# Hybrid decoder layer on one NeuronCore: values projected with the tokens moving, three heads' keys turned by VectorE blocks, turned tiles passed through DRAM

## The chip, the cores and the metric

The kernel is one launch on one core of a Trainium2 chip. The metric is the device time of that core in microseconds, as the median of several runs; before the change it is 2129.17 us over 3 runs (2129.09 to 2129.24). Beside the timed runs there is one profiled execution with its trace, in which every instruction has a line number of the kernel's source. Times of single instructions come from that execution.

## The reference

The layer works on x of 2048 tokens by 1024 features, in float32. The first part mixes tokens with two groups of heads, the second is a gated MLP with a causal convolution, and everything ends in an RMSNorm. The change touches only the first group of heads (HGRN2, a linear recurrence with four heads of key and value width 128) and the transposes that it and the attention use:

```python
u = rmsnorm(h, norm_mix_w[l])
proj = u @ w_in[l]
hq, hf, hi, hg, att = jnp.split(proj, [...], axis=-1)
f = lb + (1.0 - lb) * jax.nn.sigmoid(hf)
k_hg = (1.0 - f);  q_hg = hq * HG_DK ** -0.5;  v_hg = hi
# per head:  S_t = diag(f_t) S_{t-1} + k_t v_t^T,   o_t = S_t^T q_t
o_hg = rmsnorm(hgrn2_chunkwise(q_hg, k_hg, v_hg, log_f), hg_norm_w[l]) * silu(hg)
o_att = sliding_window_attention_with_sinks(aq, ak, av, sinks[l])
h = h + concat([o_hg, o_att]) @ w_out[l]
```

So for each head there are keys K, queries and values v over all tokens. Within chunks of 128 tokens the kernel computes products of queries and keys, and it carries a 128×128 state from chunk to chunk, for which it needs the product of a chunk's keys and values with the tokens as the summed axis.

## The kernel before

**Tiling.** The tokens are worked in two halves of 1024 (`hf` 0 and 1), each as 8 chunks of 128. Activations lie feature by token, 128 features on the partitions and 1024 tokens along the row, and there are 8 such tiles for the 1024 features. Every large product is made of three matmuls on values split into a high and a low part (`hi`, `lo`): high by high, high by low, low by high. `prep` loads a 512 KB weight tile, ACT casts the high part (line 199) and VectorE subtracts to get the low part (line 200).

**Units.** `unit` (line 203) projects the 1024 tokens of a half onto 128 output features: the weights are the stationary operand and 512 tokens move at a time, which makes 8 × 3 × 2 = 48 matmuls into two PSUM banks (line 218). Gates, forget gates (`f`), queries (`hq`), attention projections (`q`, `kv`) and the output projection (`pop`) are such units. There are four `mm` banks in PSUM, and two each of `hg` and `at`.

**Values.** `project_v` (line 670) is not a unit. It takes two heads at once, and here the tokens are stationary, so that its result has tokens on the partitions: for each of the 8 chunks, 24 matmuls with 256 weight columns moving (lines 681 to 683, tile `pvv`). ACT scales each chunk and head with the tokens' inverse norm while it copies them out of PSUM (line 685).

**A head.** `hgrn` (line 485) is a generator with five stages. `f` and `q` are units; `l` runs seven levels of pairwise products in the chunks (tiles `plev`, lines 546 to 596), in which VectorE multiplies K and Q in place after each level (lines 564, 565, 575, 576; K is final after the last line 576); `s` transposes the eight chunks of K on TensorE (tile `pkn`, line 607), copies them out with ACT (line 608, tile `Kn`, tokens on the partitions), multiplies them with the values (tile `pu`, line 614) and adds up the states (line 621); `p` makes the outputs (tile `po`, lines 634 and 639) with v and the states, and normalizes them. `gate` (line 521) is the gate's unit, run later.

**Turned tiles.** For three of the four heads the normalized output, and for three of the four attention pairs the attention weights, are transposed by `turned` (line 335) and not by TensorE: VectorE transposes all 32×32 blocks of a 128×1024 tile in one instruction (line 338), and 16 DMAs of 32 KB from SBUF to SBUF put the blocks in place (line 341). This is done for 12 tiles of attention weights and 6 of outputs.

**Order.** The stages of heads and pairs are interleaved by a list, `ORDER` (line 40): `f q l s p` are a head's stages, `qa sc pv pw` an attention pair's, `v` a `project_v`, `g` a gate, `m` a split for the output projection. A planner then lays out each engine's own instruction list when the kernel is built, from the program's order, its own costs for the instructions and the buffers that are free; on the chip each engine runs its list from front to back. All DMAs named here are issued by SyncE's queue (SP), in its list's order. Tiles with one tag share a fixed number of buffers: `t4` (2) holds Kn, the outputs and their turned form, `pp` (3) attention tiles and their turned form, `v` (2) the values.

Of the kernel before, what the change touches and what calls it, by code (L numbers as in the profile page):

```python
# [8 lines left out]
F32 = mybir.dt.float32  # L9
# [8 lines left out]
P = 128  # L18
# [20 lines left out]
UP_AFTER = 'T2'  # L39
ORDER = ("f0 q0 l0 qa0 v0 sc0 s0 p0 f1 q1 pv0 pw0 l1 qa1 sc1 f2 s1 p1 q2 pv1 pw1 l2 qa2 v1 sc2 f3 s2 p2 q3 pv2 "  # L40
         "pw2 l3 qa3 sc3 s3 p3 pv3 pw3 g0 g1 m4 m5 m6 g2 m0 m1 g3 m7 m2 m3").split()
LEVELS = [1, 2, 4, 8, 16, 32, 64]
# [3 lines left out]
VB = 2  # L46
TURNED_PAIRS = 3
TURNED_HEADS = 3


@with_exitstack
def hymba_layer(ctx: ExitStack, tc: tile.TileContext, a: dict, out: bass.AP, rows_out: bass.AP):
# [281 lines left out]

    def turned(p, tag, bufs, src, dst):

        t = p.tile([P, 4, 8, 32], F32, tag=tag, name="turn", bufs=bufs)
        nc.vector.transpose(t, src.rearrange("p n (c j) -> p c n j", j=32))
        for a in range(4):
            for c in range(4):  # L340
                nc.sync.dma_start(dst[32 * c:32 * c + 32, a], t[32 * a:32 * a + 32, c])

# [40 lines left out]
    def attend(hf, j, X, invb, KS, V, VD, mix, p):  # L383
# [9 lines left out]
        for g in range(NB):  # L393
# [48 lines left out]
            if j < TURNED_PAIRS:  # L442
                pt = p.tile([P, 4, 8, 32], F32, tag="sc", name="pt", bufs=2)
                turned(p, "pp", 3, sc.rearrange("p a b c -> p (a b) c"), pt)
                sc = pt
# [39 lines left out]
    def hgrn(hf, h, X, invb, vs, WG, gates, mix, p, fu=None):  # L485
# [114 lines left out]
        kept = TT if hf + 1 < NH else TT - 1  # L600
        Kn = p.tile([P, TT, P], F32, tag="t4", name="Kn", bufs=2)
        for b in range(NB):
            pk = ps("hg", "pkn")
            n = min(4, kept - 4 * b)
            for i in range(n):
                c = slice((b * 4 + i) * P, (b * 4 + i + 1) * P)
                nc.tensor.transpose(pk[:, i * P:(i + 1) * P], K[:, c], ident)
            nc.scalar.copy(Kn[:, 4 * b:4 * b + n].rearrange("p a b -> p (a b)"), pk[:, 0:n * P])
        SS = p.tile([P, TT, P], F32, tag="SS", name="SS", bufs=1)
        for b in range(NB):  # L610
            pu = ps("hg", "pu")
            for c in range(4 * b, min(4 * b + 4, kept)):
                i = c % 4
                marks["pu"] = nc.tensor.matmul(pu[:, i * P:(i + 1) * P], Kn[:, c], v[:, c], start=True, stop=True)
            for c in range(4 * b, min(4 * b + 4, kept)):
                i = c % 4
                if hf == 0 and c == 0:
                    nc.vector.tensor_copy(SS[:, 0], pu[:, 0:P])
                    continue
                prev = state[:, h] if c == 0 else SS[:, c - 1]  # L620
                nc.vector.scalar_tensor_tensor(SS[:, c], prev, F[:, c:c + 1], pu[:, i * P:(i + 1) * P],
                                               op0=ALU.mult, op1=ALU.add)
# [6 lines left out]
        for b in range(NB):  # L629
            at = [po[b][:, i * P:(i + 1) * P] for i in range(4)]  # L630
            empty = hf == 0 and b == 0
            for i in range(4):
                for k in range(2):
                    marks["po"] = nc.tensor.matmul(at[i][rows(k)], ST[:, k, 4 * b + i], v[:, 4 * b + i],
                                                   start=i == 0, stop=empty and i == 0, skip_group_check=True)
# [15 lines left out]
        if h < TURNED_HEADS:  # L651
            turned(p, "t4", 2, on, q.rearrange("p (a c q) -> p a c q", a=4, c=TT))
        for b, bs in halves() if h >= TURNED_HEADS else ():
# [15 lines left out]

    def project_v(hf, pr, X, rs, p):  # L670

        v = [p.tile([P, TT, P], F32, tag="v", name="v", bufs=VB) for _ in range(2)]
        parts = [prep(a["w_v"][pr, s]) for s in range(2)]
        for tt in range(TT):
            o = ps("mm", "pvv")
            t = slice(tt * P, (tt + 1) * P)
            for kt in range(KT):
                hi, lo = parts[kt // 4]
                xh, xl = X[kt]
                c = slice((kt % 4) * 256, (kt % 4 + 1) * 256)  # L680
                nc.tensor.matmul(o[:, 0:256], xh[:, t], hi[:, c], start=kt == 0, stop=False)  # L681
                nc.tensor.matmul(o[:, 0:256], xl[:, t], hi[:, c], start=False, stop=False)  # L682
                nc.tensor.matmul(o[:, 0:256], xh[:, t], lo[:, c], start=False, stop=kt == KT - 1)  # L683
            for i in range(2):
                nc.scalar.activation(v[i][:, tt], o[:, i * P:(i + 1) * P], AF.Identity, scale=rs[:, tt:tt + 1])
        return v
# [467 lines left out]
    for hf in range(NH):  # L1154
        X, kv, invb, rs, f0 = nxt
        with ExitStack() as st:
# [7 lines left out]
            for name in ORDER:  # L1164
# [9 lines left out]
                elif stage == "v":  # L1174
                    vs += project_v(hf, n, X, rs, p)
                else:
                    M[n] = split(mix[n], C.hgw if n < TURNED_HEADS else None)
# [9 lines left out]
def _layout(i):  # L1187
# [3 lines left out]
    def cols(w, idx):  # L1191
# [12 lines left out]
    w_out = i["w_out"][0][np.concatenate(rows)]  # L1204
    w_v = np.stack([cols(w_in, 1024 + pr * 256 + ar(256)).reshape(P, 2, D).transpose(1, 0, 2) for pr in range(2)])
    conv = np.concatenate([i["conv_w"][0], i["conv_b"]], 0)
# [5 lines left out]
        "w_f": np.stack([cols(w_in, 512 + h * P + ar(P)) for h in range(4)]),  # L1212
        "w_v": w_v,
        "w_g": np.stack([cols(w_in, 1536 + h * P + ar(P)) for h in range(4)]),
# [39 lines left out]
```

## Time and profile before

| | before |
|---|---|
| median of 3 runs | 2129.17 us |
| the profiled execution's own time | 2129.44 us |
| its span, first to last instruction | 2127.7 us |
| granted TensorE clock | 0.999 |
| TensorE busy (matmuls) | 2113.7 us, 99% |
| VectorE busy | 1632.4 us, 77% |
| ScalarE (ACT) busy | 1050.0 us, 49% |
| DMA | 264.34 MB, mean 124 GB/s |

The time of an execution is its span and about 1.7 us around it. "Busy" is the time in which at least one instruction of an engine was under way. Matmuls overlap each other, so the duration of one (285 to 390 ns) is longer than the distance from one to the next; the pace is read from the starts, or from the rows of the chain of waits, where each stretch of time is counted once. PE is TensorE's matmul side, PEld its weight loads, DVE VectorE, ACT ScalarE, SP SyncE and its DMA queue (SPq in rows). The mixing part of the first half runs from about 33 us to 345 us of the span, that of the second from about 1085 us to 1411 us; the rest is the MLP.

### The profile page before, as it was taken

How to read it: one execution, taken by the hardware profiler on the slowest of the kernel's cores; microseconds unless marked ns; L12 is line 12 of the kernel's file. 1: busy time of each engine (PE TensorE's matmuls, PEld its weight loads, DVE VectorE, ACT ScalarE, POOL GpSimd, SP SyncE). 2: the span in 40 equal slices, each digit the busy share in tenths (PEclk: the TensorE clock that was granted, in tenths of full speed). 3: DMA queues.
4: the chain of work that ended last, by engine and by line, in shares of the span. 5: the costliest groups of instructions: out<-in, count | busy, mean ns of one | idle time of the engine just before them, and what ended most of it. 6: DMA issues, size and time to landing. Idle time of an engine off the chain costs nothing.

```text
span 2127.7 us, 30275 instructions
## 1 busy us (share of the span) xinstructions
PE 2113.7 (99%) x11575; PEld 1763.0 (83%) x11575; DVE 1632.4 (77%) x2427; ACT 1050.0 (49%) x1855; POOL 16.9 (1%) x43
## 2 busy tenths in 40 slices
PE   8999999999999999999999999999999999999998
PEld 6988888888888888888889898888888888888887
DVE  6587786798887878785865776867988788887765
ACT  5455645564444445335635456555544444453353
POOL 2000000000000000000000000000000000000000
PEclk9999999999999999999999999999999999999999
DMA  4121213413232335964641212242223323259644
GB/s 162 42 59 45 68 52 102 136 59 121 91 124 92 98 116 168 379 235 150 216 143 40 61 38 64 60 146 97 80 99 103 110 90 124 94 194 403 228 149 134
DMA packets 105810, 264.34 MB, mean 124 GB/s; under 512 B 15808, under 2 KB 28608, under 8 KB 105664
## 3 DMA queue, kind: packets, MB, share of 16 engines
q1 hardware_dynamic: 105232, 262.14, 36.6%
q8 instruction: 91, 1.49, 0.3%
q14 instruction: 55, 0.45, 0.1%
q10 hardware_dynamic: 432, 0.27, 0.0%
HBM read 195.56 MB, written 57.34 MB: 119 GB/s over the span
## 4 chain that ended last, share of the span: by engine, by line
PE 97%; DVE 2%; DMA 1%; ACT 0%; issue 0%; SPq 0%; ACTq 0%; DVEq 0%
PE X L818 7%; PE X L816 7%; PE X L817 7%; PE pop L218 7%; PE hq L218 4%; PE q L218 4%; PE g L218 4%; PE f L218 4%; PE Y L817 4%; PE Y L818 4%; PE Y L816 4%; PE pdx L1004 3%; PE pdx L1003 3%; PE pdx L1005 3%; PE pdy L1004 3%; PE pdy L1003 3%
## 5 line engine op out<-in xcount | busy, mean ns | idle before, releaser
L689 ACT CAST whi<-raw 128x1024 fp32r<-128x1024 f32 x88 | 92.7, 1053 | 115.1 <-PE X L817 73.1
L816 PE MATMUL X<-T,whi 128*128 128x512 f32 x352 | 136.9, 389 | 0.0
L817 PE MATMUL X<-T,whi 128*128 128x512 f32 x352 | 136.9, 389 | 0.0
L818 PE MATMUL X<-T,wlo 128*128 128x512 f32 x352 | 136.9, 389 | 0.0
L887 DVE SCALAR_TENSOR_TENSOR y<-ga,cw,y 128x1024 f32<-128x1024 f32 x88 | 112.5, 1279 | 25.9 <-ACT y L885 25.9
L822 ACT COPY u<-X 128x512 f32<-128x512 f32 x88 | 51.5, 585 | 122.8 <-PE X L818 122.6
L690 DVE TENSOR_TENSOR wlo<-raw,whi 128x1024 fp32r<-128x1024 f32 x88 | 107.2, 1218 | 4.4 <-ACT whi L689 4.4
L199 ACT CAST whi<-raw 128x1024 fp32r<-128x1024 f32 x58 | 60.6, 1050 | 89.9 <-PE pop L218 36.7
L690 DVE TENSOR_TENSOR xld<-raw,xhd 128x1024 fp32r<-128x1024 f32 x72 | 80.9, 1131 | 18.3 <-ACT xhd L689 18.2
L689 ACT CAST xhd<-raw 128x1024 fp32r<-128x1024 f32 x72 | 70.0, 978 | 37.6 <-DMA raw<-act0T 12.0
L218 PE MATMUL pop<-XL,whi 128*128 128x512 f32 x256 | 82.8, 390 | 0.0
L218 PE MATMUL pop<-XH,wlo 128*128 128x512 f32 x256 | 82.6, 390 | 0.0
L218 PE MATMUL pop<-XH,whi 128*128 128x512 f32 x256 | 82.5, 391 | 0.0
L200 DVE TENSOR_TENSOR wlo<-raw,whi 128x1024 fp32r<-128x1024 f32 x58 | 70.5, 1217 | 10.4 <-ACT whi L199 10.1
L818 PEld LDWEIGHTS X<-T,wlo 128*128 128x128 f32 x352 | 66.1, 188 | 13.8
L817 PEld LDWEIGHTS X<-T,whi 128*128 128x128 f32 x352 | 66.1, 188 | 13.7
L816 PEld LDWEIGHTS X<-T,whi 128*128 128x128 f32 x352 | 66.0, 188 | 13.7
L682 PE MATMUL pvv<-whi,XL 128*128 128x256 f32 x256 | 72.7, 285 | 0.0
L681 PE MATMUL pvv<-whi,XH 128*128 128x256 f32 x256 | 72.6, 285 | 0.0
L683 PE MATMUL pvv<-wlo,XH 128*128 128x256 f32 x256 | 72.4, 287 | 0.0
L818 PE MATMUL X<-B,wlo 128*128 128x512 f32 x176 | 68.7, 390 | 0.8 <-DVE wlo L690 0.8
L817 PE MATMUL X<-T,Sh 128*128 128x512 f32 x176 | 68.6, 390 | 0.5 <-DVE T L690 0.5
(388 smaller groups left out, 6287.9 us busy)
## 6 DMA issues: line engine op xcount, KB each, us to landing
wr<-in_w_down SPq DMA_DIRECT2D x90, 512.0 KB, 5.6
raw<-in_w_gate SPq DMA_DIRECT2D x44, 512.0 KB, 3.6
raw<-in_w_up SPq DMA_DIRECT2D x44, 512.0 KB, 3.6
raw<-act0T SPq DMA_DIRECT2D x20, 512.0 KB, 5.6
raw<-act1T SPq DMA_DIRECT2D x20, 512.0 KB, 5.9
act0B<-y SPq DMA_DIRECT2D x33, 256.0 KB, 2.4
act1B<-y SPq DMA_DIRECT2D x33, 256.0 KB, 2.4
raw<-in_w_out SPq DMA_DIRECT2D x16, 512.0 KB, 3.7
```

What stands on the lines that cost most here:

```text
L218: nc.tensor.matmul(o[b], w, x[:, bs], start=f, stop=l)
L681: nc.tensor.matmul(o[:, 0:256], xh[:, t], hi[:, c], start=kt == 0, stop=False)
L682: nc.tensor.matmul(o[:, 0:256], xl[:, t], hi[:, c], start=False, stop=False)
L683: nc.tensor.matmul(o[:, 0:256], xh[:, t], lo[:, c], start=False, stop=kt == KT - 1)
L689: nc.scalar.copy(h, src)
L690: return (eng or nc.vector).tensor_tensor(l, src, h.bitcast(F32), op=ALU.subtract)
L816: nc.tensor.matmul(o, wh[:, ws], xh, start=i == 0 and not more, stop=False, skip_group_check=more)
L817: nc.tensor.matmul(o, wh[:, ws], xl, start=False, stop=False, skip_group_check=more)
L818: nc.tensor.matmul(o, wl[:, ws], xh, start=False, stop=i == 3, skip_group_check=more)
L887: nc.vector.scalar_tensor_tensor(y, g[:, w:w + HALF], C.cw[:, ft, w:w + 1], y, op0=ALU.mult, op1=ALU.add)
L1003: nc.tensor.matmul(o, wh[:, i, c], ah[:, i, cols], start=f, stop=False, skip_group_check=more)
L1004: nc.tensor.matmul(o, wh[:, i, c], al[:, i, cols], start=False, stop=False, skip_group_check=more)
```

## The change

1. `project_v` becomes a unit per head: weights stationary, tokens moving, 48 matmuls into two PSUM banks, features on the partitions. Two VectorE block transposes (one per bank, out of PSUM) and a trip through DRAM then bring the tokens onto the partitions, and eight ACT instructions scale the chunks in place. `ORDER` has `v0 v1` where `v0` stood and `v2 v3` where `v1` stood. The weights' host layout follows.
2. For heads 0 to 2 (`TURNED_KEYS = 3`) K is transposed by `turned` in place of 8 TensorE transposes and two ACT copies. The block transpose writes with a step of 8 elements, and the resulting Kn is read as weights with that step. Head 3 keeps the transposes on TensorE.
3. `turned` no longer moves blocks from SBUF to SBUF with 16 DMAs: it writes the block-transposed tile to a DRAM buffer (four of them, `DB`) with one DMA and reads it back with four, one for each quarter of the partitions. This holds for all turned tiles, the 18 there were and the new ones.

```diff
-ORDER = ("f0 q0 l0 qa0 v0 sc0 s0 p0 f1 q1 pv0 pw0 l1 qa1 sc1 f2 s1 p1 q2 pv1 pw1 l2 qa2 v1 sc2 f3 s2 p2 q3 pv2 "
-         "pw2 l3 qa3 sc3 s3 p3 pv3 pw3 g0 g1 m4 m5 m6 g2 m0 m1 g3 m7 m2 m3").split()
+ORDER = ("f0 q0 l0 qa0 v0 v1 sc0 s0 p0 f1 q1 pv0 pw0 l1 qa1 sc1 f2 s1 p1 q2 pv1 pw1 l2 qa2 v2 v3 sc2 f3 s2 p2 q3 pv2 pw2 l3 qa3 sc3 s3 p3 pv3 pw3 g0 g1 m4 m5 m6 g2 m0 m1 g3 m7 m2 m3").split()
...
+TURNED_KEYS = 3
+DB = 4
...
-    def turned(p, tag, bufs, src, dst):
+    def flat(t):
+
+        return t.rearrange("p a b c -> p (a b c)")
+
+    def turned(p, tag, bufs, src, dst, strided=False):
 
         t = p.tile([P, 4, 8, 32], F32, tag=tag, name="turn", bufs=bufs)
-        nc.vector.transpose(t, src.rearrange("p n (c j) -> p c n j", j=32))
-        for a in range(4):
-            for c in range(4):
-                nc.sync.dma_start(dst[32 * c:32 * c + 32, a], t[32 * a:32 * a + 32, c])
+        tv = t.rearrange("p c n i -> p c (n i)").rearrange("p c (i n) -> p c n i", n=8) if strided else t
+        for i, s in enumerate(src):
+            n = 8 // len(src)
+            nc.vector.transpose(tv[:, :, i * n:(i + 1) * n], s.rearrange("p (n c j) -> p c n j", n=n, j=32))
+        d = dp.tile([P, 4, 256], F32, tag="turned", name="turned", bufs=DB)
+        nc.sync.dma_start(d.rearrange("p c x -> p (c x)"), flat(t))
+        for c in range(4):
+            nc.sync.dma_start(dst[32 * c:32 * c + 32].rearrange("p a b c -> p a (b c)"),
+                              d[:, c].rearrange("(a j) x -> j a x", a=4))
...
-        Kn = p.tile([P, TT, P], F32, tag="t4", name="Kn", bufs=2)
-        for b in range(NB):
+        if h < TURNED_KEYS:
+            Kt = p.tile([P, 4, 32, TT], F32, tag="t4", name="Kt", bufs=2)
+            turned(p, "t4", 2, [K], Kt, True)
+            Kn = Kt.rearrange("p a i n -> p n (a i)")
+        else:
+            Kn = p.tile([P, TT, P], F32, tag="t4", name="Kn", bufs=2)
+        for b in range(NB) if h >= TURNED_KEYS else ():
             pk = ps("hg", "pkn")
...
-                marks["pu"] = nc.tensor.matmul(pu[:, i * P:(i + 1) * P], Kn[:, c], v[:, c], start=True, stop=True)
+                marks["pu"] = nc.tensor.matmul(pu[:, i * P:(i + 1) * P], Kn[:, c], v[:, :, c], start=True, stop=True)
...
-    def project_v(hf, pr, X, rs, p):
-
-        v = [p.tile([P, TT, P], F32, tag="v", name="v", bufs=VB) for _ in range(2)]
-        parts = [prep(a["w_v"][pr, s]) for s in range(2)]
-        for tt in range(TT):
-            o = ps("mm", "pvv")
-            t = slice(tt * P, (tt + 1) * P)
-            for kt in range(KT):
-                hi, lo = parts[kt // 4]
-                xh, xl = X[kt]
-                c = slice((kt % 4) * 256, (kt % 4 + 1) * 256)
-                nc.tensor.matmul(o[:, 0:256], xh[:, t], hi[:, c], start=kt == 0, stop=False)
-                nc.tensor.matmul(o[:, 0:256], xl[:, t], hi[:, c], start=False, stop=False)
-                nc.tensor.matmul(o[:, 0:256], xh[:, t], lo[:, c], start=False, stop=kt == KT - 1)
-            for i in range(2):
-                nc.scalar.activation(v[i][:, tt], o[:, i * P:(i + 1) * P], AF.Identity, scale=rs[:, tt:tt + 1])
+    def project_v(h, X, rs, p):
+
+        o = unit(a["w_v"][h], X, "vT")
+        v = p.tile([P, 4, TT, 32], F32, tag="v", name="v", bufs=VB)
+        turned(p, "pp", 3, o, v)
+        for c in range(TT):
+            nc.scalar.activation(v[:, :, c], v[:, :, c], AF.Identity, scale=rs[:, c:c + 1])
         return v
```

The other two callers of `turned` pass a list of one flattened tile, the second use of v (`po`, line 634) reads `v[:, :, c]` as well, and the host layout of `w_v` is one tile per head.

More of the change, by code (lines that the diff above doesn't have):

```diff
@@ L443, in attend @@
                 pt = p.tile([P, 4, 8, 32], F32, tag="sc", name="pt", bufs=2)
-                turned(p, "pp", 3, sc.rearrange("p a b c -> p (a b) c"), pt)
+                turned(p, "pp", 3, [sc.rearrange("p a b c -> p (a b c)")], pt)
                 sc = pt
@@ L633, in hgrn @@
                 for k in range(2):
-                    marks["po"] = nc.tensor.matmul(at[i][rows(k)], ST[:, k, 4 * b + i], v[:, 4 * b + i],
+                    marks["po"] = nc.tensor.matmul(at[i][rows(k)], ST[:, k, 4 * b + i], v[:, :, 4 * b + i],
                                                    start=i == 0, stop=empty and i == 0, skip_group_check=True)
@@ L651, in hgrn @@
         if h < TURNED_HEADS:
-            turned(p, "t4", 2, on, q.rearrange("p (a c q) -> p a c q", a=4, c=TT))
+            turned(p, "t4", 2, [on.rearrange("p c t -> p (c t)")], q.rearrange("p (a c q) -> p a c q", a=4, c=TT))
         for b, bs in halves() if h >= TURNED_HEADS else ():
@@ L1174, in hymba_layer @@
                 elif stage == "v":
-                    vs += project_v(hf, n, X, rs, p)
+                    vs.append(project_v(n, X, rs, p))
                 else:
@@ L1204, in _layout @@
     w_out = i["w_out"][0][np.concatenate(rows)]
-    w_v = np.stack([cols(w_in, 1024 + pr * 256 + ar(256)).reshape(P, 2, D).transpose(1, 0, 2) for pr in range(2)])
     conv = np.concatenate([i["conv_w"][0], i["conv_b"]], 0)
@@ L1212, in _layout @@
         "w_f": np.stack([cols(w_in, 512 + h * P + ar(P)) for h in range(4)]),
-        "w_v": w_v,
+        "w_v": np.stack([cols(w_in, 1024 + h * P + ar(P)) for h in range(4)]),
         "w_g": np.stack([cols(w_in, 1536 + h * P + ar(P)) for h in range(4)]),
```

## The prediction

> **What bounds the kernel now.** I read the page first: busy time by engine and the chain that ended last.
>
> ```profile
> span 2127.7 us, 30275 instructions
> PE 2113.7 (99%) x11575; PEld 1763.0 (83%) x11575; DVE 1632.4 (77%) x2427; ACT 1050.0 (49%) x1855; POOL 16.9 (1%) x43
> PE 97%; DVE 2%; DMA 1%; ACT 0%; issue 0%; SPq 0%; ACTq 0%; DVEq 0%
> ```
>
> TensorE carries 97% of the chain, so time is gained or lost by what TensorE must do and by holes cut into it. Then I asked for the busy times in the two stretches in which the edited code runs (first half of the tokens, then second half), and for TensorE's own waits.
>
> ```profile
> 44.00:335.00 291.00, 290.95 (x2335) 249.12 (x2334) 220.14 (x409) 166.27 (x421) 0.52 (x1) 1.00 0.19 56
> 1097.00:1400.00 303.00, 303.00 (x2394) 258.75 (x2394) 219.38 (x400) 167.10 (x419) 1.05 (x2) 1.00 0.20 60
> PE poT L471 <- DVE po L463: 0.2, 1, 0.2
> ```
>
> The columns are length, then busy time of PE, PEld, DVE, ACT and POOL, granted clock, DMA share and GB/s. TensorE has no hole in 594 us, at clock 1.00; VectorE is busy 439.5 us of them (74%), the 16 DMA engines a fifth. The wait shown, 0.2 us, is the only one of TensorE that stands behind a turned tile today, with 18 tiles turned. So here a microsecond taken from TensorE is a microsecond gained, as long as what is added elsewhere arrives in time.
>
> **TensorE's part: values.** The counts and the durations of the touched work come from the groups, the pace from the chain in order of time (start, length, what).
>
> ```profile
> L682 PE MATMUL pvv<-whi,XL 128*128 128x256 f32 x256 | 72.7, 285 | 0.0
> L607 PE MATMUL pkn<-ident,K x60: 270/272/273, 98.1 to 1381.5; 128*128 128x128 f32 x60
> L685 ACT ACTIVATE v<-pvv,y x64: 344/360/369, 76.4 to 1277.6; 128x128 f32<-128x128 f32 x64
> L608 ACT COPY Kn<-pkn x16: 471/576/626, 99.1 to 1383.2; 128x512 f32<-128x512 f32 x12, 128x384 f32<-128x384 f32 x4
> L338 DVE STREAM_TRANSPOSE turn<-sc 128x1024 f32<-128x1024 f32 x12 | 14.9, 1239 | 0.0
> L741 DVE TENSOR_TENSOR h<-h,pop 128x512 f32<-128x512 f32 x32 | 20.8, 682 | 31.1 <-PE pop L218 31.1
> ```
>
> ```profile
> 92.49 0.12 PE pvv L683
> ...
> 97.17 0.12 PE pvv L683
> 98.23 0.87 PE pkn L607 x8
> ...
> 358.36 60.79 PE pop L218 x268
> ...
> 1150.84 0.76 PE pkn L607 x7
> ...
> 1188.65 6.37 PE q L218 x27
> ...
> 1327.97 10.43 PE g L218 x46
> ```
>
> Today three lines of 256 matmuls each, 768 in all, have tokens stationary and 256 weight columns moving. Between the first and the last pvv row lie 39 steps without a break: (97.17 − 92.49) / 39 = 0.120 us each, so 768 × 0.120 = 92.2 us. The change makes them ordinary units: weights stationary, 512 tokens moving, 48 matmuls for each of 8 head-halves, 384 in all, with the same product count. The trace has that form: 60.79 / 268 = 0.2268 and 10.43 / 46 = 0.2267 us, so 384 × 0.2268 = 87.1 us. Saving: 5.1 us. Twice the columns cost less than twice the time, because half as many instructions and weight loads pay their fixed part.
>
> The Trainium skill ("TensorE: Matmul & The Clock Gate", section "Back-to-back issue gap") speaks against most of this: by its warm gap, N/2.4 + 2.5 ns, 256 columns take 109.2 and 512 take 215.8 ns. By it 768 would take 83.9 and 384 would take 82.9 us, a saving of 1.0 instead of 5.1. The rows above, 120 and 227 ns, differ from it, and I go by them.
>
> **TensorE's part: keys.** The transposes of K go away for three of four heads. A group of eight takes 0.87 us in the first half, one of seven 0.76 us in the second: 3 × 0.87 + 3 × 0.76 = 4.9 us. They stand in the chain between other matmuls, so this is path time. Two ACT copies a head and half go with them, 12 of 16, 12 × 0.576 = 6.9 us off the path (ACT is a little over half busy).
>
> **What comes in: VectorE.** Sixteen transposes of 128×512 from PSUM (two per head and half). The trace has none from PSUM; the two bounds are half of the 1.24 us transpose, 0.62, and the PSUM-reading addition, 0.68. I take 0.68: 10.9 us. Six of K at 1.24: 7.4 us. VectorE rises from 439.5 to about 458 of 594 us, 77%. Its cover is its own idle time; without it, all 18 us would show. The 64 scalings of v stay on ACT, at 0.36 us each, now out of SBUF and behind a DMA.
>
> **What comes in: the trip through DRAM.** Now 8 value tiles and 6 key tiles are turned beside the 18 of today, 32 trips, each one write of 512 KB, a wait of SP for its landing, and four reads of 128 KB. First the issues (count, KB each, median us to landing) and the timeline of SP, then the timeline of VectorE and the chain at pu.
>
> ```profile
> 117.34 10.08 SPq L341 DMA_DIRECT2D pt<-turn  x16
> pt<-turn SPq DMA_DIRECT2D x192, 32.0 KB, 1.8
> keep<-h SPq DMA_DIRECT2D x32, 256.0 KB, 2.1
> act0T<-T SPq DMA_DIRECT2D x22, 256.0 KB, 3.1
> raw<-in_w_f SPq DMA_DIRECT2D x8, 512.0 KB, 3.6
> 98.11 0.33 SPq L198 DMA_DIRECT2D raw<-in_w_f  x1
> 92.24 0.69 DVE L576 TENSOR_TENSOR K<-K,F 128x512 f32<-128x512 f32 x1
> 174.11 0.68 DVE L576 TENSOR_TENSOR K<-K,F 128x512 f32<-128x512 f32 x1
> 235.34 0.68 DVE L576 TENSOR_TENSOR K<-K,F 128x512 f32<-128x512 f32 x1
> 104.14 0.22 PE pu L614 x2
> 184.38 1.78 PE pu L614 x16
> 248.29 1.34 PE pu L614 x12
> ```
>
> SP today spends 10.08 us issuing the 16 small DMAs of one tile, 0.63 each, 18 × 10.1 = 182 us. A trip of the new kind holds SP for 0.33 (issue of a 512 KB transfer), the write's landing (2.1 to 3.6 by the rows; I take 3.0) and four issues of 0.33 to 0.63 (I take 0.63, the nearest shape): 5.9 us, 32 × 5.9 = 187 us. SP's load is as before, in shorter holds. Queued behind the new wait are the weight loads; ACT's casts wait for those, and the units for the casts. On ACT the scalings of v now wait for a read, with casts and level copies queued behind them; ACT is idle for 261 of the 594 us, which covers it.
>
> A key tile's whole trip: transpose 1.24, SP 5.9, landing of the last read 1.8 to 3.6 (I take 2.5), together 9.6 us; by the bounds 6.8 to 11.2 us. K is final at the end of line 576 and is read first by pu: the gaps today are 104.14 − 92.93 = 11.2, 184.38 − 174.79 = 9.6 and 248.29 − 236.02 = 12.3 us, while the transposes and copies that they hold need only about 2. So even with TensorE's order kept, the trip about fits; what hides it is the unit matmuls that already stand there. Without that cover it would cost 6 × 9.6 = 58 us. A value tile's trip, with half a transpose more and eight scalings of 0.36 us behind it, takes about 13 us; head 0's unit ends about 11 us (48 × 0.227) before today's pair does (at 97.3), and heads 1 and 3 are read a whole head later than 0 and 2. The 18 old tiles land sooner than today (9.6 against 1.24 + 10.1 + 1.8 = 13.1 us); nothing on TensorE waits there, so I book no gain. For late arrivals I take 1.0 us, between 0.4 (today's 0.2 us of 18 trips, for 32) and 4.
>
> **Strides.** Kn is now read as weights with a step of 8 floats, and the K transpose writes with that step. No row has such a step; the nearest are the level operations, whose step is 2 floats at the first level and whose runs grow.
>
> ```profile
> 65.27 1.49 DVE L584 COPY_PREDICATED ST<-lmask,plev 64x256 f32<-64x256 uint32 x2
> ...
> 76.49 0.90 DVE L584 COPY_PREDICATED ST<-lmask,plev 64x256 f32<-64x256 uint32 x2
> 69.44 0.62 PE plev L558 x16
> ...
> 82.40 0.61 PE plev L558 x16
> ```
>
> The predicated copy takes 1.49 us for two with short runs, 0.90 with longer ones, a factor of 1.66; the level matmuls, whose moving operand has the same steps, take 0.62 and 0.61. So the K transpose lies between 1.24 and 2.1 us (hidden), and 45 weight loads of about 0.109 us (0.87 / 8, the same stationary shape) cost between nothing and 45 × 0.072 = 3.2 us more. I take nothing, since the row of TensorE shows nothing.
>
> The Trainium skill ("SBUF — State Buffer", section "Specifications (TRN2)") gives 16-byte lines, with a penalty for each access that crosses to a new one; a step of 32 bytes crosses each time. No row here has that step on TensorE, so this is the first rival.
>
> **Sum.** −5.1 − 4.9 + 1.0 = −9.0 us. The profiled execution took 2129.44 us (span 2127.7 and 1.7 around it), so 2120.4; the median of the runs lies 0.27 lower, 2120.2 us. With late arrivals from 0 to 4 and no penalty, 2119 to 2123; the saving may be a microsecond or two larger where a break in the stream goes too.
>
> **Rivals.**
> 1. *Strided weights cost.* At half pace on 45 loads, 45 × 0.109 = 4.9 us: 2125.1, no change that can be told (0.2%, 4.3 us, is about what a measurement tells here). At a third of the pace, 2130. For it: the predicated copy's factor. Against: the level matmuls.
> 2. *The unit doesn't run at its best pace.* The row of 27 q matmuls gives 6.37 / 27 = 0.236 us where small matmuls cut in. At that pace 384 take 90.6 us, the saving is 1.6, and the time 2123.7. Against: pvv is cut in the same places today.
> 3. *The key trip comes late: slower.* Place: pu of heads 0 to 2 in both halves. SP runs in order, and its loads wait for their buffers:
>
> ```profile
> SPq L198 <- DVE wlo L200: 255.1, 31, 25.9
> ```
>
> That is 8.2 us on average. A write or read of a key tile queued behind such a load makes the trip 9.6 + 8.2 = 17.8 us against a gap of about 11, 6.8 us of a standing TensorE, as its list is fixed. At three of the six places, +20: 2120.2 + 20 = 2140; at all six 2161. It decides from 9 us in all, 1.5 us a key tile. For it: gap and trip are of one size, and SP now also waits for landings. Against: the same queue carries 18 longer trips and TensorE loses 0.2 us.
> 4. *The change doesn't do what it says*, for instance keys turned but pu held back to the same place, with other waits filling the room: 2129. Against: TensorE's list has no hole to grow into, and the removed matmuls are certain.
>
> **Chances.** Forecast 0.60 (own range 2116 to 2124); rival 1 0.15, mostly at 2125; rival 2 0.08; rival 3 0.13; rival 4 0.04. Faster takes the forecast, rival 2 and a third of rival 1: 0.72. Within 0.2%: most of rival 1, rival 4 and the mild end of rival 3: 0.15. Slower: 0.13. The range runs from 2115 to 2131: below it lies an underestimate of the saving, above it rival 3.
>
> **What would show it.** Right: pvv rows are gone and a v unit shows 48 matmuls of 512 at 0.227 us in the chain; pkn groups only for head 3; pu groups of eight still at 0.9 us; TensorE without holes in both stretches and with no wait for Kn or v over 1 us; the mixing stretch about 5 us shorter in each half. Rival 1 shows in the weight load and pace of pu, rival 2 in the v units' pace, rival 3 in TensorE's waits at pu. Wrong beyond these: a hole outside the two stretches.

## The result: 4.1% slower, with the profile after

The changed kernel takes 2216.58 us (median of 4 runs, 2216.35 to 2217.63) against 2129.20 us before (4 runs, 2129.09 to 2129.45): a ratio of 1.0411, 95% interval 1.0393 to 1.0429, or +87.4 us. The forecast was 2120.2 us and its range ended at 2131.

The page of the changed kernel, with the busy times and the shares of the chain of waits:

```profile
span 2214.8 us, 29325 instructions
...
PE 2137.2 (96%) x11146; PEld 1763.4 (80%) x11146; DVE 1654.5 (75%) x2449; ACT 1045.5 (47%) x1843; POOL 17.7 (1%) x43
...
PE 85%; DVE 8%; ACT 3%; DMA 2%; issue 1%; SPq 1%; DVEq 0%; ACTq 0%
```

TensorE has 429 matmuls fewer than before (11146 against 11575) and yet 23.5 us more busy time, and its share of the chain fell from 97 to 85%. So two things are new: slower work on TensorE, and holes.

Where they lie shows in three landmarks of TensorE's timeline: the starts of the last output projection (`pop`) of the first half, of the last `kv` of the second half (just behind the first half's MLP), and of the last `pop` of the second half. The rows of these tiles before (columns: duration min/median/max in ns, then the first and the last start):

```profile
L218 PE MATMUL pop<-XH,whi x128: 387/389/481, 335.5 to 429.4; 128*128 128x512 f32 x128
...
L218 PE MATMUL kv<-XL,whi x64: 388/389/632, 6.8 to 1084.4; 128*128 128x512 f32 x64
...
L218 PE MATMUL pop<-XH,whi x128: 387/389/499, 1385.1 to 1484.4; 128*128 128x512 f32 x128
```

and after:

```profile
L219 PE MATMUL pop<-XH,whi x128: 387/389/797, 352.1 to 474.9; 128*128 128x512 f32 x128
...
L219 PE MATMUL kv<-XL,whi x64: 388/389/629, 7.2 to 1129.9; 128*128 128x512 f32 x64
...
L219 PE MATMUL pop<-XH,whi x128: 387/389/794, 1454.9 to 1572.3; 128*128 128x512 f32 x128
```

At the first landmark the kernel is 45.5 us late, at the second still 45.5, at the third 87.9. The MLP is unchanged; all of the loss is in the two mixing stretches. The busy times up to these landmarks (length, then PE, PEld, DVE, ACT, POOL, granted clock, DMA share, GB/s), before:

```profile
44.00:429.50 385.50, 385.45 (x2809) 327.24 (x2808) 280.21 (x510) 213.07 (x505) 0.52 (x1) 1.00 0.23 72
1084.50:1485.00 400.50, 400.34 (x2884) 339.48 (x2883) 284.71 (x512) 217.53 (x508) 2.09 (x4) 1.00 0.25 77
```

and after:

```profile
44.00:475.00 431.00, 399.09 (x2590) 328.47 (x2590) 290.04 (x520) 210.02 (x498) 0.52 (x1) 0.95 0.30 92
1130.00:1573.00 443.00, 410.87 (x2671) 337.62 (x2670) 296.32 (x524) 215.68 (x503) 2.08 (x4) 0.95 0.31 97
```

The two stretches grew by 88 us, from 786 to 874. TensorE now stands for 64.0 us of them (874.0 − 810.0), where it stood for 0.2, and is busy for 24.2 us more, with a granted clock of 0.95 instead of 1.00. The longest of TensorE's own waits name the place:

```profile
PE poT L481 <- DVE po L463: 22.9, 5, 12.6
PE poT L481 <- DMA pt<-turned: 11.7, 4, 4.0
...
PE pu L629 <- DMA Kt<-turned: 1.6, 1, 1.6
```

More than half of the 64 us, 34.6, stand at `poT`, the product of the attention weights with the values, and only 1.6 at `pu`, where the turned keys are read; the rest is spread over many lines, none above 6 us. The keys are nevertheless the first suspect, as their path shows: VectorE's timeline, SP's, and the chain at head 0's `pu`.

```profile
101.07 2.17 DVE L346 STREAM_TRANSPOSE turn<-K 128x1024 f32<-128x1024 f32 x1
...
142.18 0.80 SPq L348 DMA_DIRECT2D turned<-turn  x2
...
146.75 2.05 SPq L350 DMA_DIRECT2D Kt<-turned  x4
...
154.43 4.02 PE pu L629 x16
```

K is turned by 103.24 us, but its write to DRAM is issued at 142.18, together with one of attention pair 0's tiles. TensorE's list has `pu` at 154.4, where it was at 104 before, and fills the 50 us with work of later stages (`hq`, `q` and `f` of what comes next). That this work is missing further on is my reading; the experiments below test it. In the window of the first long hole (columns as above), and at the first matmul behind it:

```profile
194.00:224.00 30.00, 18.46 (x156) 15.22 (x154) 18.45 (x34) 10.99 (x31) 0.00 (x0) 0.80 0.57 169
...
217.74 0.70 PE L481 MATMUL poT<-po,VD 128*64 128x128 f32 x4 [8.53 <-DVE po L463]
```

TensorE works 18.5 of 30 us there, at a clock of 0.80. The last column of the second row says that it had stood for 8.53 us. What the lower clock does shows in one kind of work, 28 `poT` matmuls in a row, first in a full stretch and then right behind these waits (rows of the chain):

```profile
148.41 1.68 PE poT L481 x28
...
225.39 3.26 PE poT L481 x28
```

The second takes almost twice as long.

### The profile page after: what moved, and what is told of

Read it like the earlier page. It is cut to its first block, busy times and chain, and to the rows that moved or that the text cites. A ratio compares the mean times of both kernels' runs of the same rounds, so it can differ in the third digit from the quotient of the medians.

```text
span 2214.8 us, 29325 instructions
## 1 busy us (share of the span) xinstructions
PE 2137.2 (96%) x11146; PEld 1763.4 (80%) x11146; DVE 1654.5 (75%) x2449; ACT 1045.5 (47%) x1843; POOL 17.7 (1%) x43
## 4 chain that ended last, share of the span: by engine, by line
PE 85%; DVE 8%; ACT 3%; DMA 2%; issue 1%; SPq 1%; DVEq 0%; ACTq 0%
PE X L824 7%; PE X L823 7%; PE X L822 7%; PE pop L219 6%; PE vT L219 4%; PE Y L823 4%; PE Y L824 4%; PE Y L822 4%; PE f L219 3%; PE pdx L1010 3%; PE pdx L1011 3%; PE pdx L1009 3%; PE q L219 3%; PE hq L219 3%; PE pdy L1010 3%; PE pdy L1009 3%
## 5 line engine op out<-in xcount | busy, mean ns | idle before, releaser
L822 PE MATMUL X<-B,whi 128*128 128x512 f32 x176 | 68.7, 391 | 0.0
L822 PE MATMUL Z<-B,whi 128*128 128x512 f32 x176 | 68.7, 390 | 0.0
L824 PE MATMUL Z<-B,wlo 128*128 128x512 f32 x176 | 68.6, 390 | 0.0
```

Source lines behind the costliest of these rows:

```text
L822: nc.tensor.matmul(o, wh[:, ws], xh, start=i == 0 and not more, stop=False, skip_group_check=more)
L824: nc.tensor.matmul(o, wl[:, ws], xh, start=False, stop=i == 3, skip_group_check=more)
```

## The experiments

A time stands beside the kernel before in the same set of runs, 2128.8 to 2129.4 us. The kernels with 32 buffers, with the old values, with the units apart and with unit-step keys in the changed kernel were run twice each, the others 4 to 10 times. Each edit makes the planner lay out all engines' lists anew.

### One part at a time

**Without the turned keys.**

```diff
-TURNED_KEYS = 3
+TURNED_KEYS = 0
```

> The changed kernel with all four heads' keys back on TensorE (TURNED_KEYS = 0); the values as units and the DRAM trip stay. Theory A, the values: a v unit holds two of the four mm banks until VectorE turns it, the turn waits for one of the three pp buffers that attention holds, and no other unit can start meanwhile. By it most of the loss stays: 2170 to 2190 us. Theory B, the keys: the trip of K stands in front of pu and the strided weights make pu slow (4.0 against 1.8 us a head). By it the loss goes with the keys and the 5 us of the values are won: 2122 to 2130 us. Theory C, the DRAM trip of the old 18 tiles is slower for its readers than the moves from SBUF to SBUF: 2150 us or more here, and the same in the run that changes the trip alone.

Measured: 2135.77 us, ratio 1.0033 (1.0021 to 1.0046). Without the turned keys 80.8 of the 87.4 us are gone. What remains is a loss of 7.0 us, where values alone were forecast to gain 5.1; so theory B's range was missed, though it comes nearest.

**The 18 old tiles through DRAM, nothing else.** `project_v`, `ORDER` and the keys are as before.

```diff
-        for a in range(4):
-            for c in range(4):
-                nc.sync.dma_start(dst[32 * c:32 * c + 32, a], t[32 * a:32 * a + 32, c])
+        d = dp.tile([P, 4, 256], F32, tag="turned", name="turned", bufs=DB)
+        nc.sync.dma_start(d.rearrange("p c x -> p (c x)"), flat(t))
+        for c in range(4):
+            nc.sync.dma_start(dst[32 * c:32 * c + 32].rearrange("p a b c -> p a (b c)"),
+                              d[:, c].rearrange("(a j) x -> j a x", a=4))
```

> The kernel before with nothing changed but the way of the 18 tiles that it turned already: one write to DRAM and four reads in place of 16 moves. Theories A and B: 2126 to 2131 us, no hole on TensorE. Theory C: 2150 us or more, TensorE waits at poT for pt.

Measured: 2132.59 us, 1.0019 (1.0010 to 1.0029). The trip costs 3.8 us where I had booked nothing, 1.6 over the range of theories A and B; theory C's 2150 is out.

**The values' units, all tiles moved from SBUF to SBUF** (the changed kernel without turned keys and with the 16 DMAs of before in `turned`).

```diff
-TURNED_KEYS = 3
+TURNED_KEYS = 0
...
-        d = dp.tile([P, 4, 256], F32, tag="turned", name="turned", bufs=DB)
...
+        for a in range(4):
+            for c in range(4):
+                nc.sync.dma_start(dst[32 * c:32 * c + 32, a], t[32 * a:32 * a + 32, c])
```

> Values as units, no keys turned, and every turned tile moved by 16 DMAs from SBUF to SBUF as in the kernel before. Theory A: as slow as with the DRAM trip or slower, 2170 to 2210 us, since the banks and pp buffers are held longer (10 us of issues for a tile). Theory B: 2122 to 2130 us. Theory C: 2122 to 2130 us here and slow with the DRAM trip.

Measured: 2149.71 us, 1.0098 (1.0083 to 1.0113). The units lose 21 us without any DRAM trip, less than theory A's range and more than the others'. Their eight tiles add 16 moves each to SP here, so this isn't the price of the units alone.

**The keys alone**: old values, the 18 old tiles by 16 moves, only the three keys through DRAM.

```diff
+        if not strided:
+            for a in range(4):
+                for c in range(4):
+                    nc.sync.dma_start(dst[32 * c:32 * c + 32, a], t[32 * a:32 * a + 32, c])
+            return
         d = dp.tile([P, 4, 256], F32, tag="turned", name="turned", bufs=DB)
```

> The kernel before with three heads' keys turned through DRAM alone; values and the 18 other tiles as before. Theory B, by the pace of pu alone: 2129 - 4.9 + 90 x 0.14 = 2137 us, and with TensorE standing at pu for the trip 2150 to 2180 us. Theory A: not above 2137 us, with no hole on TensorE. Theory C: the same as A, as only 6 tiles go through DRAM.

Measured: 2137.73 us, 1.0042 (1.0027 to 1.0057). That is +9.0 us, not +80, and what theory B had for the pace of `pu` alone (2137). The timelines of VectorE, SP and TensorE at head 0 show the trip as it was forecast:

```profile
92.53 2.15 DVE L347 STREAM_TRANSPOSE turn<-K 128x1024 f32<-128x1024 f32 x1
...
94.71 0.33 SPq L354 DMA_DIRECT2D turned<-turn  x1
...
97.34 1.75 SPq L356 DMA_DIRECT2D Kt<-turned  x4
...
104.72 3.97 PE L635 MATMUL pu<-v,Kt 128*128 128x128 f32 x16
```

The write follows the transposition at once, and `pu` starts at 104.72, where it was before (103.98). The last of the four reads, issued at 98.7, lands 2.8 us later, so the trip takes about 9.0 us from the start of the transposition (forecast 9.6), and 12.2 us pass up to the first `pu`: it is hidden, and TensorE has no wait for Kt in this run. Two things follow: the trip as such does not explain the 87 us, and the keys still lose 9 us here without a hole. Of these, 7.7 are the pace of `pu`, which takes 3.97 us for 16 matmuls: 12.6 us more in all (worked out under the strides), less the 4.9 of the transposes.

### The 80 us: who shares the DRAM buffers

**The changed kernel with the old `project_v` and `ORDER`.**

```diff
-    def project_v(h, X, rs, p):
+    def project_v(hf, pr, X, rs, p):
```

> The changed kernel with the values projected as before: keys turned and all turned tiles through DRAM. Theory D, the loss beyond the parts needs the v units: 2138 to 2146 us (2129 + 3.4 + 9 = 2141). Theory F, keys and pairs on one queue with waits for landings are enough: 2170 us or more.

Measured: 2183.34 us, 1.0254 (1.0224 to 1.0283). The loss doesn't need the values' units: keys (+9.0) and old tiles (+3.8) alone make 12.8 in separate kernels and 53.9 in one. In the timelines of VectorE and SP the write is late again:

```profile
92.42 2.15 DVE L347 STREAM_TRANSPOSE turn<-K 128x1024 f32<-128x1024 f32 x1
...
140.13 0.80 SPq L349 DMA_DIRECT2D turned<-turn  x2
```

**32 DRAM buffers in place of 4.**

```diff
-DB = 4
+DB = 32
```

> The changed kernel with 32 DRAM buffers for turned tiles in place of 4, so that no write waits for the reads of an earlier tile. Theory E, the ring of DRAM buffers couples values, keys and pairs: 2140 to 2160 us, near the sum of the parts alone (2129 + 3.4 + 3.2 + 9 = 2145). Theory D: unchanged, 2210 to 2222 us.

Measured: 2213.89 us, 1.0397 (1.0367 to 1.0427), and head 0's key is written at 142.23 us instead of 142.18. With 32 buffers for 32 tiles no write has to wait for an earlier tile's reads, so it is not a lack of buffers.

**The units of heads 2 and 3 apart from each other.**

```diff
-... l2 qa2 v2 v3 sc2 f3 s2 ...
+... l2 qa2 v2 sc2 f3 v3 s2 ...
```

> The changed kernel with the stages v2 and v3 apart: v3 after sc2 and f3 in place of right behind v2, so that the two units need not hold all four mm banks at one time. Theory D: a good part of the loss goes, 2150 to 2195 us, and the hole of about 9 us in front of poT after the v units shrinks. Theories E and F: 2205 us or more.

Measured: 2210.41 us, 1.0381 (1.0351 to 1.0411). The time is nearly the same, and head 0's key is written at 142.85, as late as before. But the holes are elsewhere: TensorE waits 19.9 us at `g` for VectorE's `turn`, and at `poT` behind `po` only 2.8 instead of 22.9. So setting the units apart is no remedy, while this run alone doesn't show that the units have no part in the holes.

**A DRAM tag for each kind of tile** (values, attention weights, keys, outputs), four buffers each.

```diff
-        d = dp.tile([P, 4, 256], F32, tag="turned", name="turned", bufs=DB)
+        d = dp.tile([P, 4, 256], F32, tag="turned" + kind, name="turned", bufs=DB)
```

> The changed kernel with one edit: the DRAM buffer of a turned tile has a tag of its own for each kind (keys, values, outputs, attention weights) in place of one tag for all. Theory G: buffers of one tag are handed out in the program's order, and the program has pair 0's second tile ahead of head 0's keys; so the keys' write, whose block transpose ended at 103 us, was put on SP behind that tile's write at 142 us, and head 0's pu came at 154 in place of 104 us. By it the write follows its transpose within 3 us, head 0's pu comes at 104 to 108 us, the holes of 8 us and more go, and the time falls to the sum of the parts alone: 2129 + 3.4 + 3.2 + 9 = 2145 us (2140 to 2152). Theory D (banks of the v units) and theory F (SP's waits for landings): 2200 us or more, and the holes stay.

Measured: 2146.78 us, 1.0088 (1.0072 to 1.0105): 69.8 us less than the changed kernel. Its busy times, and VectorE's, SP's and TensorE's timelines:

```profile
PE 2118.3 (99%) x11146; PEld 1747.9 (82%) x11146; DVE 1652.1 (77%) x2449; ACT 1046.1 (49%) x1843; POOL 18.2 (1%) x43
...
101.56 2.21 DVE L346 STREAM_TRANSPOSE turn<-K 128x1024 f32<-128x1024 f32 x1
...
103.80 0.34 SPq L348 DMA_DIRECT2D turned<-turn  x1
106.61 1.74 SPq L350 DMA_DIRECT2D Kt<-turned  x4
...
113.01 3.86 PE L629 MATMUL pu<-v,Kt 128*128 128x128 f32 x16
```

The same transposition, half a microsecond later than in the changed kernel, is now followed by its write at 103.80 instead of 142.18, and `pu` comes at 113.0 instead of 154.4 (theory G had 104 to 108). Theories D and F, 2200 us or more, are out as they stood. TensorE's 11146 matmuls, as many as in the changed kernel, keep it busy for 2118.3 us instead of 2137.2: of the 73.7 us between the two profiled spans (2214.8 and 2141.1), 18.9 were slower work and the rest holes. So what decides is whether the kinds of tiles share one tag, whatever its number of buffers. The edit parts all four kinds at once; the run with the old values shows that the values aren't needed for the late write, and keys and attention tiles alone weren't tried. It fits an assignment of a tag's buffers in the order of the program: `ORDER` has `sc0`, which asks for pair 0's two tiles, ahead of `s0`, which asks for the key's. The key is ready first, and its write stands behind tiles that are turned up to 40 us later. That this is the planner's rule, and that the late `pu` is what opens the holes, is inferred from these kernels; a trace doesn't show it.

### The strides

**Unit-step keys by one ACT copy**, in the changed kernel.

```diff
-            Kn = Kt.rearrange("p a i n -> p n (a i)")
+            Kn = p.tile([P, TT, P], F32, tag="t4", name="Kn", bufs=2)
+            nc.scalar.copy(Kn, Kt.rearrange("p a i n -> p n (a i)"))
```

> The changed kernel, but ACT copies the turned keys into a tile with unit steps (one more instruction of about 1 us for each of 6 head-halves), so the weights of pu have no step. If the strided weights alone make pu slow: pu of a turned head at 1.8 us again in place of 4.0, TensorE's work 12 us less, and if nothing else moves 2203 to 2208 us. If the step isn't the cause of pu's pace, pu stays at 4.0 us and the time at 2216 to 2222 us. By theory D (holes: v2 and v3 hold all four mm banks while the keys and pairs pass through their buffers) the holes stay.

Measured: 2187.25 us, 1.0272 (1.0242 to 1.0302), 29.3 us less than the changed kernel. That is more than the step was expected to give (9 to 14 us), and head 0's key is written as late as before, at 142.15; where the rest comes from wasn't followed up.

**The same on top of the tag for each kind** (this edit and the one before it together).

> Own tags, and ACT's copy that gives the keys unit steps. If what is left of the keys' cost is the weights' step: 12 us less than with own tags alone, about 2133 us, and pu of a turned head at 1.8 us. If the trip itself costs, less than 6 us of it go.

Measured: 2138.48 us, 1.0048 (1.0033 to 1.0063), 8.3 us less than with strided keys (2146.78), where 12 were expected; ACT has six more copies. The runs with strided keys lie between 2142.8 and 2149.0 us, so 8.3 is good to a few microseconds. Within the changed kernel the weight loads of `pu` stand side by side, three heads strided (`Kt`) and one not (`Kn`):

```profile
L629 PEld LDWEIGHTS pu<-v,Kt x90: 312/336/339, 154.4 to 1419.6; 128*128 128x128 f32 x90
...
L629 PEld LDWEIGHTS pu<-v,Kn x30: 186/192/193, 387.9 to 1492.2; 128*128 128x128 f32 x30
```

A load takes 336 ns against 192. Sixteen `pu` take 4.02 us against 1.78 before, 0.251 against 0.111 us each, so 90 of them cost 90 × 0.140 = 12.6 us more. This agrees with the Trainium skill ("SBUF — State Buffer", section "Specifications (TRN2)"), by which SBUF is read in lines of 16 bytes and each access that crosses into a new one pays.

**A tag for each kind and no turned keys** (that edit with `TURNED_KEYS = 0`).

> Own tags and all keys on TensorE. Theory G: the shared tag also held up tiles without the keys, so this is under the 2135.8 us of the shared tag, 2124 to 2132 us. If the loss of 7 us there was the values' or the trip's own: 2134 to 2137 us.

Measured: 2142.34 us, 1.0063 (1.0048 to 1.0078). Against it, unit-step turned keys gain 3.9 us (2138.48), near the 4.9 forecast for the transposes, and strided ones lose 4.4 (2146.78); in both comparisons the intervals overlap, so neither is shown. It is also 6.6 us above the kernel with one tag and no keys (2135.77): separate tags are no gain by themselves, and other lists alone move the time by several microseconds. Both expectations, 2124 to 2132 and 2134 to 2137, were missed.

### The values: who holds the PSUM banks

**Units and their DRAM trip, all else as before.** Only values go through DRAM, the rest by 16 moves, with keys transposed on TensorE (`TURNED_KEYS = 0`).

```diff
+        if kind != "v":
+            for a in range(4):
+                for c in range(4):
+                    nc.sync.dma_start(dst[32 * c:32 * c + 32, a], t[32 * a:32 * a + 32, c])
+            return
         d = dp.tile([P, 4, 256], F32, tag="turned" + kind, name="turned", bufs=DB)
```

> The kernel before with the values alone changed: units, turned through DRAM; the 18 other tiles by 16 moves, keys on TensorE. By the prediction's term for the values, 5.1 us less work for TensorE: 2124 to 2126 us. If the v units lose what they save (banks held, ACT waiting): 2129 to 2136 us.

Measured: 2144.72 us, 1.0076 (1.0061 to 1.0091): +15.7 us, where −5.1 was forecast, and above both expectations. The rows of the chain, of VectorE's timeline, of two windows and of TensorE's waits:

```profile
227.09 1.24 DVE po L468
...
228.35 2.51 DVE L346 STREAM_TRANSPOSE turn<-vT 128x512 f32<-128x512 f32 x4
...
231.63 3.63 PE f L219 x14
...
194.00:224.00 30.00, 26.79 (x237) 21.78 (x235) 22.93 (x50) 13.52 (x46) 0.00 (x0) 1.00 0.18 48
...
224.00:254.00 30.00, 27.86 (x214) 23.22 (x215) 17.48 (x31) 14.90 (x38) 0.00 (x0) 0.89 0.41 110
...
PE plev L573 <- DVE Q L580: 8.6, 4, 3.2
```

Heads 2 and 3's units fill all four `mm` banks, and VectorE turns the four banks (x4) in one go right behind the second `po` of pair 1. Only then does the next unit, `f`, go on, at 231.63. `po` waits for the 16 moves of its attention tile, and the turned values share tag `pp` with it: the same pattern as above, this time in SBUF, with PSUM held meanwhile. TensorE's own waits stand at the level products in front of `f`, for VectorE's Q; that the banks keep `f` from filling them is inferred from the tags, and no row shows a wait for a bank.

**The turned values from another tag**, that of the raw weight tiles: first in the kernel above, then without turned keys, then in the whole change with unit-step keys, the latter two with a DRAM tag for each kind.

```diff
-        turned(p, "pp", 3, o, v, kind="v")
+        turned(wp, "raw", RAW, o, v, kind="v")
```

> The values' units as in the kernel of before plus units through DRAM (2144.7 us), with one edit: the values' turned tile comes from the ring of the weights' raw tiles (3 buffers) and no longer from the three buffers that the softmax stages' pt and po share with it. Theory H: buffers of one tag are handed out in program order, so the turn of v2 and v3 stands on VectorE behind pair 1's second po (228.35 behind 227.09), and the four banks that the units filled by 218 stay held until then; each half loses about 10 us so. By H the turn moves ahead of that po, the hole goes, and the time is 2124 to 2130 us. Rival U (the units themselves or the trip cost, wherever the turn stands): 2140 to 2146. Rival W (the raw ring, now shared, makes the weights' loads late): above 2146.

> The changed kernel with a DRAM tag for each kind of tile and no turned keys (2142.3 us), with the same edit: the values' turned tile from the raw ring. Theory H: 2124 to 2132 us. Rival U: 2138 to 2143. Rival W: above 2143.

> The whole change with a DRAM tag for each kind of tile and the keys copied to unit step by ScalarE (2138.5 us), with the same edit: the values' turned tile from the raw ring. Theory H: 2120 to 2128 us, which would be at or below the kernel before. Rival U: 2134 to 2139. Rival W: above 2139.

Measured: 2168.34 (1.0188, 1.0173 to 1.0203), 2156.83 (1.0134, 1.0119 to 1.0150) and 2161.30 us (1.0151, 1.0135 to 1.0166). All three are slower than with `pp`, by 23.6, 14.5 and 22.8 us; the times lie where rival W had them. VectorE's, SP's, ACT's and TensorE's timelines of the first:

```profile
210.65 0.72 DVE L346 STREAM_TRANSPOSE turn<-vT 128x512 f32<-128x512 f32 x1
...
217.07 10.02 SPq L350 DMA_DIRECT2D hg<-turn  x16
227.14 2.66 SPq L355 DMA_DIRECT2D v<-turned  x4
229.85 0.43 SPq L199 DMA_DIRECT2D raw<-in_w_v  x1
...
235.05 1.03 ACT L200 CAST whi<-raw 128x1024 fp32r<-128x1024 f32 x1
...
236.13 1.22 PE L219 MATMUL vT<-XH,whi 128*128 128x512 f32 x2 [2.88 <-ACT whi L200]
```

The turn does move ahead, to 210.65 from 228.35. But the next values' weights are now loaded only at 229.85, behind the turned tile's reads, which stand on SP behind 16 moves of an output. So these kernels couldn't tell whether the units cost by themselves.

**The units turned into the values' own tile**, which is written to DRAM and read back into place, so that no buffer of another tag is asked for. Two kernels have it: one with the values' units alone, and one with the whole change, unit-step keys and a tag for each kind.

```diff
-        t = p.tile([P, 4, 8, 32], F32, tag=tag, name="turn", bufs=bufs)
+        t = p.tile([P, 4, 8, 32], F32, tag=tag, name="turn", bufs=bufs) if bufs else dst
...
-        turned(p, "pp", 3, o, v, kind="v")
+        turned(p, "", 0, o, v, kind="v")
```

> The values' units through DRAM, all else by 16 moves (2144.7 us), with one edit: VectorE turns the unit into the values' own tile v, which goes to DRAM and is read back into the same v, so that no buffer of another tag is asked for. Theory H (the units' banks are held because the turned tile waits for its turn in a shared tag; moving it to the raw ring freed the banks but held the weights' loads instead, 2168.3): with neither ring touched 2126 to 2134 us. Rival U (the units or the trip cost wherever the turn stands): 2140 to 2146. A middle value, 2134 to 2140, would say that the wait moves to the v tile itself, of which there are two.

> The whole change with a DRAM tag for each kind of tile and unit-step keys by ScalarE (2138.5 us), with the same edit: the units turned into the v tile itself. Theory H: 2120 to 2130 us, about the kernel before or below. Rival U: 2135 to 2140. Middle (v tiles are late): 2130 to 2135.

Measured: the first takes 2125.68 us, ratio 0.9986 (0.9976 to 0.9996), 19.0 us less than with the turned tile in `pp` and 0.3 under theory H's 2126 to 2134. It is 3.1 us under the kernel before, the only version here below it; that lies inside the 0.2% that I had set as telling, though the interval excludes 1. Its page, the busy times in the two stretches and VectorE's timeline:

```profile
PE 2108.0 (99%) x11191; PEld 1739.8 (82%) x11191; DVE 1640.3 (77%) x2443; ACT 1049.2 (49%) x1855; POOL 17.6 (1%) x43
...
44.00:335.00 291.00, 290.02 (x2122) 238.59 (x2121) 221.73 (x413) 164.03 (x412) 0.52 (x1) 1.00 0.26 72
1097.00:1400.00 303.00, 301.54 (x2235) 247.73 (x2234) 223.90 (x418) 168.99 (x435) 0.52 (x1) 1.00 0.25 72
...
208.36 1.31 DVE L346 STREAM_TRANSPOSE v<-vT 128x512 f32<-128x512 f32 x2
...
222.27 1.31 DVE L346 STREAM_TRANSPOSE v<-vT 128x512 f32<-128x512 f32 x2
```

The two heads are turned 14 us apart, each soon after its unit, the hole is gone (2.4 us idle in the 594), and TensorE's busy time is 5.7 us below that of before (2113.7). So the units don't cost by themselves; what did was where they are turned to. The run doesn't separate the banks that came free sooner from the `pp` buffers, which the attention tiles now have to themselves.

The second takes 2135.54 us, 1.0035 (1.0021 to 1.0049): 2.9 us less than with `pp` (2138.48, the two ranges overlap), and still 6.7 above the kernel before. Theory H's 2120 to 2130 was missed here, and the time lies in rival U's range. TensorE's waits show where tiles come late even so, the keys' copies at `pu` and attention tiles at `poT`:

```profile
PE pu L630 <- ACT Kn L615: 4.4, 5, 1.6
PE poT L481 <- DMA pt<-turned: 2.9, 2, 1.8
PE poT L481 <- DVE po L463: 2.7, 2, 2.2
```

They make 10.0 us, more than the 4.9 us of transposes that the turned keys save.

**The 18 old tiles through DRAM with a tag for each kind** (the second experiment's kernel with that edit).

> The kernel before with its 18 turned tiles through DRAM (2132.6 us with one DRAM tag), with a DRAM tag for each kind of tile. If the shared tag makes those 3.6 us: 2129 to 2130 us. If the trip itself makes them (write landing and reads in place of one move): 2132 to 2133.

Measured: 2130.49 us, 1.0009 (0.9999 to 1.0018). With own tags the trip can't be told from the 16 moves. It is 2.1 us less than with the shared tag, but the two intervals overlap.

## Why the prediction was wrong, step by step

The route from the changed kernel back, one edit on top of the other: 2216.58, a DRAM tag for each kind 2146.78, unit-step keys 2138.48, values turned in place 2135.54, before 2128.8. By these runs 69.8 us come from the shared DRAM tag, 8.3 from strides, 2.9 from the values' SBUF tag (not clear of the noise), and 6.7 are left. In another order the pieces have other sizes (unit steps gained 29.3 us while the tag was shared, the values in place 19.0 where the keys stayed on TensorE).

1. **What bounds the kernel: right.** TensorE had no slack, so every hole became time.
2. **Values, −5.1: the size of the work was right, the path was not.** In the chain of the changed kernel a unit's stretches read:

```profile
75.42 5.21 PE vT L219 x22
...
204.97 3.62 PE vT L219 x16
```

These are 0.237 us a matmul between level products, which is rival 2's pace, and 0.226 in the other, the pace I took. TensorE's busy time decides: it fell by 5.7 us in the kernel that has the units alone and in place, and 3.1 of them showed in its time. The warm gap that the prediction set against this, from the Trainium skill ("TensorE: Matmul & The Clock Gate", section "Back-to-back issue gap"), is called there the gap of a single, isolated matmul, so it was no figure for a stream. What failed is that I priced a unit by its matmuls only. A `pvv` chunk held one bank and ACT emptied it; a unit holds two until VectorE has turned them, and two heads in a row hold all four. Which buffer that turn waits for, and behind what, wasn't asked. That was worth 20.8 us between forecast and measurement (+15.7 against −5.1).
3. **Keys, −4.9: plausible, and outweighed.** Unit-step turned keys gain 3.9 us over transposed ones in the same surroundings, within overlapping intervals. But I took nothing for strided weights, by the level matmuls, whose *moving* operand has the steps. The measured price is 12.6 us of TensorE's work. Rival 1 had the mechanism right and two sizes wrong: it counted 45 loads at half the pace, where 90 stand (two for each chunk: 16 for a head in the first half, 14 in the second, three heads), at 2.26 times the old time each. The upper bound of 3.2 us in the paragraph on strides, by a factor of 1.66, was too low by a factor of four.
4. **VectorE: the sizes right, the cover only in part.** 16 transposes from PSUM take 0.63 us each in a row of four and 0.72 alone (0.68 taken), those of K 2.0 to 2.2, at the upper bound of 2.1 (the sum had 1.24). In the kernel with the keys alone no transposition stands in the chain of the mixing stretches; in the changed kernel two of the keys' do in each half, at 1.9 to 2.1 us each.
5. **The trip, 9.6 us against gaps of about 11: right on the chip, wrong in the list.** Alone, the key's trip takes about 9.0 us and leaves `pu` where it was. The step that failed is "late arrivals, 1.0 us, between 0.4 and 4": the sum took for granted that the planner issues a write right behind its transposition. I had read that tiles with one tag share buffers, and that each engine runs its list in order, but didn't ask in which order tiles of four kinds with one tag get those buffers. It was the mis-sized term: 69.8 us by the run with a tag for each kind, against 1.0 in the sum.
6. **Rival 3 named the place and the sign,** keys late on SP with TensorE's list fixed, at 2140 to 2161. Its cause, queueing behind loads of 8.2 us, was wrong: the write stood for 39 us behind other turned tiles, and TensorE's list was not fixed either. It was laid out anew with `pu` 50 us later, so the wait showed at `poT` and not at `pu`, where I said to look.
7. **The 18 old tiles, 0:** +3.8 us with the shared tag, and with tags of their own +1.7, not to be told from nothing.

Open: the 6.7 us that remain with all three causes eased. The waits at `pu` and `poT` above are where they show, and their causes weren't separated. Nor was it tried which part of the 3.1 us of the best version comes from the units and which from another list; the 6.6 us between two kernels that differ only in tags warns of that.

## What to carry to other kernels

Before a change adds a tile to a tag, list who else draws from it and in what order the program asks: a tile that is ready early waits behind one that is asked for earlier and ready late, and more buffers in the same tag need not help. Price a moved product by what it holds until it is emptied (banks, buffers, the queue of the emptying engine) as well as by its matmuls; here turning into the destination's own tile asked for no other tile's buffer, and won back 19.0 us where the units stood alone, though only 2.9 in the whole change. When an operand gets a new step, look for a row in which the same kind of operand has that step, since a moving operand without penalty says nothing of weights.

## What the runs showed of the hardware that was not expected

- FP32 weights with a step of 32 bytes: 336 ns a load against 192, and 0.251 us a matmul against 0.111 in a row of 16. The moving operand of the level matmuls shows nothing at a step of 8 bytes.
- VectorE's 128×1024 transpose takes 2.0 to 2.2 us when it writes with that step, against 1.24.
- The granted clock falls with the holes: 0.80 in the 30 us in which TensorE worked 18.5, and 0.95 over both stretches. 28 `poT` matmuls took 3.26 us right behind a hole and 1.68 in a full stretch, and the same number of matmuls kept TensorE busy for 18.9 us less once most holes were gone. So in these runs a hole costs more than its own length.
